# A tile scheduler that orders instructions by a finer simulator

## The chip, the core and the metric

The kernel runs on one core of one Trainium2 chip. A core has four compute engines that run side by side, each with its own list of instructions in a fixed order: TensorE (PE) multiplies matrices, with its loads of the fixed operand listed as PEld; VectorE (DVE) and ScalarE (ACT) work on elements; GpSimd (POOL) does some element work too. SyncE (SP) issues most transfers. An engine takes its instructions strictly as they are listed, and where one has to wait for another engine or for a transfer, all that stands behind it waits too. The time is that of one execution on the device in microseconds (us); of several runs the median is taken.

## The reference

The model has two layers, over 1024 tokens and 16 learned ones ahead of them (1040 in all), with 1024 features:

```python
merged = jnp.concatenate([rms_norm(o_sb, sb_norm_g), rms_norm(o_s5, s5_norm_g)], axis=-1)   # layer 0
return merged.astype(h.dtype) @ w_out
...
v_new = val_c - jnp.einsum('bhcd,bhde->bhce', kcd_c, state)                                 # layer 1
o_c = jnp.einsum('bhcd,bhde->bhce', qg_c, state) + jnp.einsum('bhcs,bhse->bhce', intra_c, v_new)
state = state * jnp.exp(gl_c)[..., None, None] + jnp.einsum('bhcd,bhce->bhde', kt_c, v_new)
...
return jnp.square(jax.nn.relu(h @ w1)) @ w2                                                 # after each mixer
```

Layer 0 mixes tokens by stick-breaking attention (8 heads of 64 features) and by an S5 state space model; layer 1 by a gated DeltaNet with 8 heads of 128 features: a causal convolution and a silu give queries, keys and values, a triangular system is solved within each chunk of tokens, and the state of a head goes from chunk to chunk. Behind each mixer stands an MLP of 4096 hidden features. All is in fp32.

## The kernel before

Features lie in the partitions, tokens along the rows. A large product (`unit`, L167) is cut into output tiles of 128 features by 336 to 352 tokens. Each operand is split into a high and a low part, and three matmuls (L174, L175, L176) for each of eight tiles of 128 input features add up in one of three PSUM banks named mm. Weights come by SP into wraw (two buffers), and DVE (L163) and POOL or DVE (L164) make whi and wlo of them.

The stages in the order of time, by the profile: projections and S5 of layer 0 and its attention (0 to 750 us), the MLP of layer 0 (to 1500), the DeltaNet mixer (1500 to 2250), and the MLP of layer 1. The mixer, `mixer1` (L1564), has two parts that matter here.

The preparation, about 1560 to 1850 us. For each head the products of `conv_in` (L1178) go from their PSUM bank to cx by DVE (L1189). `conv_silu` (L1195) makes cy of it: ACT scales (L1199), DVE adds three shifted copies (L1205), ACT applies the silu (L1206). `decays` (L1219) loads rows named grow, adds a mask (L1228 on POOL, L1229 on DVE) and takes exponentials (L1231 on ACT). `keys` (L1236) and `queries` (L1304) transpose cy on PE (L1251, L1266, L1315) and multiply it with itself (L1288, L1328). `solve` (L1340) inverts 128 triangular blocks of 32 x 32 on DVE, by 31 pairs of L1350 and L1351, once for heads 0 to 3 and once for heads 4 to 7; `combine` (L1384) makes inverses of 128 x 128 blocks of them.

The chain, about 1850 to 2175 us. `chain` (L1469) goes through the nine chunks of a head, one head after the other. A step takes the state S through PE (L1492), DVE (L1494, rho), PE (L1497), ACT (L1499, xc), PE (L1503) and DVE (L1508), which gives the next S; L1513 and L1514 on PE make the step's output. Each of these matmuls is of 128 x 128 fp32 values, which PE takes in two passes. Beside the chain stand the products for the gates and the values of later heads, `combine`, and `gated` (L1535, with transposes L1556).

The program writes its instructions out in Python: generators (strands) of one kind of work are stepped while another kind is emitted, with a clock of its own (`pause`, L111, and the constants C1, C2, C3 in the chain, J1 to J4 elsewhere). That gives a program order. The tile context at L1903 then decides the real order: it knows which instruction needs which, simulates the engines, and at each point lets an engine take, of the instructions that are ready in the simulated time, the one that comes first in program order. The buffers of the pools are given out as this goes. Which instruction counts as ready, and so what stands ahead of what on each engine, depends on the durations and delays that the simulator assumes. What one instruction waits for on the chip is set by the data and the buffers, not by the simulated times.

## Time and profile before

| | |
|---|---|
| runs, us | 3028.56, 3016.03, 3018.09 |
| median, us | 3018.09 |
| profiled execution, span from first to last instruction, us | 3011.3 |
| mean granted clock of PE in it | 0.948 |
| ACT busy, us (share) | 892.8 (30%) |
| POOL busy, us (share) | 864.6 (29%) |
| instructions of PE, DVE, ACT, POOL | 17628, 3158, 1934, 628 |

The span is the profiled execution's own time; the median of the runs is 6.8 us above it. Busy shares are means over the whole program, in which the stages differ, so a stage is read by a window of its own. A wait is listed with the engine and line that waited, and the last thing that it waited for. The granted clock is the share of PE's full clock that the chip let it have: at 0.50 a matmul takes twice its time.

### The profile page before, as it was taken

The page shows a single profiled execution, that of the slowest core. Times are in us where ns is not written, and L with a number is a line of the kernel's source. Part 1 is how long each engine was busy: PE and PEld are TensorE (multiplying, and loading weights), DVE is VectorE, ACT ScalarE, POOL GpSimd, SP SyncE. Part 2 cuts the span into 40 slices and gives each one's busy share as a digit, 9 for nine tenths or more (in the row PEclk, how much of TensorE's full clock was granted, in tenths as well). Part 3 has the DMA queues.
Part 4 walks back from the last instruction along what each step waited for, and adds up shares of the span by engine and source line. Part 5 has one row for each costly group of instructions (what it writes and reads, how often), then busy time and mean ns, then how long its engine had stood idle before and what let it go on. Part 6 is the DMA issues. An engine that isn't in the chain of part 4 may idle for free. (4 is left out here: it accounts for less than half of the span.)

```text
span 3011.3 us, 44561 instructions
## 1 busy us (share of the span) xinstructions
PE 2838.4 (94%) x17628; PEld 2685.8 (89%) x17628; DVE 1773.1 (59%) x3158; ACT 892.8 (30%) x1934; POOL 864.6 (29%) x628
## 2 busy tenths in 40 slices
PE   7899998999999999999896978999989999999998
PEld 7688667888999999999886978899988999999997
DVE  8633778667455555555646995545546455555555
ACT  4112566554311101111435423334434111111112
POOL 5551225225311221222522132211143222122123
PEclk9989567889999999999998999999999999999999
DMA  3435212134111111111426666453332111111113
GB/s 126 158 127 161 71 43 92 41 104 146 58 50 43 50 46 46 50 42 51 130 85 201 220 205 208 157 153 110 127 106 84 50 50 43 50 50 43 50 50 112
DMA packets 168289, 284.92 MB, mean 95 GB/s; under 512 B 40880, under 2 KB 108672, under 8 KB 168080
## 3 DMA queue, kind: packets, MB, share of 16 engines
q1 hardware_dynamic: 164192, 277.38, 28.8%
q10 hardware_dynamic: 3888, 4.69, 0.4%
q8 instruction: 139, 2.28, 0.3%
q14 instruction: 70, 0.57, 0.1%
HBM read 204.80 MB, written 77.21 MB: 94 GB/s over the span
## 5 line engine op out<-in xcount | busy, mean ns | idle before, releaser
L174 PE MATMUL mm<-ahi,whi 128*128 128x344 f32 (+2 forms) x2592 | 862.4, 333 | 33.5 <-DVE cx L1189 22.1
L164 POOL TENSOR_TENSOR wlo<-wraw,whi 128x1024 fp32r<-128x1024 f32 x181 | 439.5, 2430 | 1504.1 <-DVE whi L163 1138.1
L176 PE MATMUL mm<-ahi,wlo 128*128 128x344 f32 (+2 forms) x2592 | 844.9, 326 | 1.8 <-DVE wlo L164 1.8
L175 PE MATMUL mm<-hl,whi 128*128 128x344 f32 (+4 forms) x1920 | 619.1, 322 | 0.0
L174 PEld LDWEIGHTS mm<-ahi,whi 128*128 128x128 f32 x2592 | 497.2, 192 | 41.7 <-DVE cx L1189 23.3
L176 PEld LDWEIGHTS mm<-ahi,wlo 128*128 128x128 f32 x2592 | 497.0, 192 | 4.5 <-DVE wlo L164 2.9
L176 PE MATMUL mm<-hh,wlo 128*128 128x344 f32 (+4 forms) x1536 | 492.8, 321 | 2.9 <-POOL wlo L164 2.9
L408 DVE TENSOR_TENSOR acc<-mm,acc 128x344 f32<-128x344 f32 (+4 forms) x672 | 343.9, 515 | 253.4 <-PE mm L176 253.4
L174 PE MATMUL mm<-hh,whi 128*128 128x344 f32 (+4 forms) x1536 | 492.0, 320 | 0.1
L385 ACT ACTIVATE t<-t 128x344 f32<-128x344 f32 (+2 forms) x192 | 94.4, 492 | 1093.7 <-DVE t L384 1093.7
L175 PEld LDWEIGHTS mm<-hl,whi 128*128 128x128 f32 x1920 | 363.8, 189 | 1.3 <-issue 0.6
L175 PE MATMUL mm<-ml,whi 128*128 128x344 f32 (+2 forms) x1056 | 340.1, 322 | 0.7 <-DVE ml L227 0.7
L163 DVE CAST whi<-wraw 128x1024 fp32r<-128x1024 f32 x181 | 180.0, 997 | 196.7 <-PE mm L175 160.6
L176 PEld LDWEIGHTS mm<-hh,wlo 128*128 128x128 f32 x1536 | 289.2, 188 | 3.8 <-POOL wlo L164 3.5
L174 PEld LDWEIGHTS mm<-hh,whi 128*128 128x128 f32 x1536 | 289.5, 188 | 0.9 <-DVE acc L408 0.3
L227 DVE TENSOR_TENSOR hl<-t,hh 128x344 fp32r<-128x344 f32 (+2 forms) x192 | 162.2, 845 | 166.6 <-ACT hh L226 165.5
L175 PE MATMUL mm<-mh,whi 128*128 128x344 f32 (+2 forms) x768 | 246.8, 321 | 0.0
L175 PEld LDWEIGHTS mm<-ml,whi 128*128 128x128 f32 x1056 | 199.7, 189 | 1.1 <-DVE ml L227 1.0
L384 DVE SCALAR_TENSOR_TENSOR t<-mm,rb 128x344 f32<-128x344 f32 (+2 forms) x192 | 98.5, 513 | 121.0 <-PE mm L176 121.0
L175 PEld LDWEIGHTS mm<-mh,whi 128*128 128x128 f32 x768 | 144.6, 188 | 0.5 <-issue 0.2
L175 PE MATMUL mm<-hh,whi 128*128 128x344 f32 (+2 forms) x384 | 126.7, 330 | 0.0
L853 DVE TENSOR_TENSOR_SCAN keep<-keep,cst 128x400 f32<-128x400 f32 (+5 forms) x72 | 95.5, 1338 | 45.8 <-ACT keep L851 45.4
(425 smaller groups left out, 4530.0 us busy)
## 6 DMA issues: line engine op xcount, KB each, us to landing
wraw<-w SPq DMA_DIRECT2D x128, 512.0 KB, 3.5
wraw<-wino SPq DMA_DIRECT2D x32, 512.0 KB, 3.7
dm<-dmd SPq DMA_DIRECT2D x16, 520.0 KB, 4.8
hsd<-hs SPq DMA_DIRECT2D x48, 172.0 KB, 1.8
wraw<-wine SPq DMA_DIRECT2D x12, 512.0 KB, 3.7
wraw<-qkd SPq DMA_DIRECT2D x8, 520.0 KB, 3.6
acc<-acc SPq DMA_DIRECT2D x8, 520.0 KB, 4.6
dmd<-grow SPq DMA_DIRECT2D x8, 520.0 KB, 5.3
```

The lines of the kernel that those rows point to most:

```text
L163: nc.vector.tensor_copy(hi[:, :n], raw[:, :n])
L164: (nc.vector if fast else nc.gpsimd).tensor_sub(lo[:, :n], raw[:, :n], f(hi[:, :n]))
L174: nc.tensor.matmul(pt, wh, h[:, o:o + n], start=i == 0, stop=False)
L175: nc.tensor.matmul(pt, wh, l[:, o:o + n], start=False, stop=False)
L176: nc.tensor.matmul(pt, wl, h[:, o:o + n], start=False, stop=i == len(kts) - 1)
L227: (lo_eng or nc.vector).tensor_sub(lo, src, f(hi))
L384: nc.vector.scalar_tensor_tensor(t1[:, :n], pt, 0.0, st["rb"][:, o:o + n], op0=ALU.max, op1=ALU.mult)
L385: nc.scalar.activation(t2[:, :n], t1[:, :n], AF.Square)
L408: nc.vector.tensor_add(acc[m][:, o:o + n], pt, acc[m][:, o:o + n])
L853: v.tensor_tensor_scan(kp[:n, 0:L][:, ::-1], kp[:n, 0:L][:, ::-1], self.one_row[:n, :L], 1.0, op0=ALU.mult, op1=ALU.mult)
```

## The change

One argument of the tile context:

```diff
-    with _tile.TileContext(nc) as tc:
+    with _tile.TileContext(nc, schedule_with_timeline_sim=True) as tc:
```

(All other lines of the diff take out docstrings and comments; line numbers stay.) The scheduler uses its finer simulator, so the simulated times at which instructions become ready differ, and with them the order on each engine and the buffers given out. What is computed, and by which instructions, stays.

The order of PE's rows in the two MLPs (800 to 1400 and 2300 to 2900 us) is the same as before. Rows move in layer 0's mixer, and most in the DeltaNet mixer. ACT has 42 loads of a function table in place of 52. Three places are shown; in each row stand the line, the operation, output<-inputs by their names in the program with buffer numbers, the shape, and xN where rows of one kind follow each other.

The first is PE in the chain, one step and the start of the next. The names are those of `chain`: S is the state, ch a slot with a head's operands, rho and xc the values between the links. Before:

```order
L1492 MATMUL tr_18472<-S_18464,ch_18313 128x128
L174 MATMUL mm_18458<-ahi_13100,whi_18053 128x344
L175 MATMUL mm_18458<-hh_12777,whi_18053 128x344
L176 MATMUL mm_18458<-ahi_13100,wlo_18054 128x344
L174 MATMUL mm_18458<-ahi_13101,whi_18053 128x344
L175 MATMUL mm_18458<-hl_12778,whi_18053 128x344
L176 MATMUL mm_18458<-ahi_13101,wlo_18054 128x344
L1497 MATMUL tr_18496<-rho_18474,ch_18313 128x128
```

The same step in the changed order, on to the next products:

```order
L1492 MATMUL tr_18472<-S_18464,ch_18313 128x128
L1513 MATMUL ax_18510<-S_18464,ch_18319 128x128
L1497 MATMUL tr_18496<-rho_18474,ch_18313 128x128
L1503 MATMUL tr_18506<-xc_18498,ch_18316 128x128
L1514 MATMUL ax_18510<-xc_18498,ch_18316 128x128
L1492 MATMUL tr_18516<-S_18508,ch_18313 128x128
L1513 MATMUL ax_18510<-S_18508,ch_18319 128x128
L1497 MATMUL tr_18535<-rho_18518,ch_18313 128x128
L1503 MATMUL tr_18551<-xc_18537,ch_18316 128x128
L1514 MATMUL ax_18510<-xc_18537,ch_18316 128x128
L174 MATMUL mm_18759<-ahi_13098,whi_18526 128x352
L175 MATMUL mm_18759<-hh_12472,whi_18526 128x352
```

Product rows stood between the links of a step; now two whole steps follow each other with no product row, and the products stand behind them in a row.

The second is DVE near 1590 us, where the products of the convolution are evicted (L1189, cx from an mm bank) beside the convolution of other heads (L1205, cy) and the mask of the decays (L1229, grow). Before:

```order
L1229 TENSOR_TENSOR grow_14268<-grow_14268,cst_63 16x16
L163 CAST whi_14726<-wraw_14724 128x1024
L1189 TENSOR_TENSOR cx_14302<-mm_14304,rb_13107 128x352
L1189 TENSOR_TENSOR cx_14302<-mm_14351,rb_13107 128x344
L1205 SCALAR_TENSOR_TENSOR cy_14341<-cx_13696,gains_64,cy_14341 128x1040 x2
L1205 SCALAR_TENSOR_TENSOR cy_14363<-cx_13698,gains_64,cy_14363 128x1040
L1205 SCALAR_TENSOR_TENSOR cy_14341<-cx_13696,gains_64,cy_14341 128x1040
L1205 SCALAR_TENSOR_TENSOR cy_14363<-cx_13698,gains_64,cy_14363 128x1040
L1229 TENSOR_TENSOR grow_14381<-grow_14381,cst_63 16x16
L1189 TENSOR_TENSOR cx_14302<-mm_14388,rb_13107 128x344
```

And in the changed order:

```order
L1229 TENSOR_TENSOR grow_14268<-grow_14268,cst_63 16x16
L1189 TENSOR_TENSOR cx_14302<-mm_14304,rb_13107 128x352
L1189 TENSOR_TENSOR cx_14302<-mm_14351,rb_13107 128x344
L163 CAST whi_14932<-wraw_14930 128x1024
L1189 TENSOR_TENSOR cx_14302<-mm_14388,rb_13107 128x344
L1205 SCALAR_TENSOR_TENSOR cy_14341<-cx_13696,gains_64,cy_14341 128x1040 x3
L1205 SCALAR_TENSOR_TENSOR cy_14363<-cx_13698,gains_64,cy_14363 128x1040 x3
L1229 TENSOR_TENSOR grow_14381<-grow_14381,cst_63 16x16
```

The third eviction, of mm_14388, moved ahead of six rows L1205 and of the mask add of grow_14381; a weight's cast (whi_14932) moved ahead of it.

The third is DVE near 1760 us, in the second half's solve (sU_16026), where cx_16094 is evicted. Before:

```order
L1350 TENSOR_TENSOR sprod_16034<-sU_16026,sN_16025 128x192
L1351 TENSOR_TENSOR sU_16026<-sU_16026,sprod_16034 128x8x24
L1350 TENSOR_TENSOR sprod_16034<-sU_16026,sN_16025 128x207
L1351 TENSOR_TENSOR sU_16026<-sU_16026,sprod_16034 128x9x23
L1350 TENSOR_TENSOR sprod_16034<-sU_16026,sN_16025 128x220
L1351 TENSOR_TENSOR sU_16026<-sU_16026,sprod_16034 128x10x22
L1350 TENSOR_TENSOR sprod_16034<-sU_16026,sN_16025 128x231
L1189 TENSOR_TENSOR cx_16094<-mm_16096,rb_13107 128x352
L1189 TENSOR_TENSOR cx_16094<-mm_16126,rb_13107 128x344
```

And in the changed order:

```order
L1351 TENSOR_TENSOR sU_16026<-sU_16026,sprod_16034 128x4x28
L1205 SCALAR_TENSOR_TENSOR cy_16082<-cx_15477,gains_64,cy_16082 128x1040
L1320 TENSOR_SCALAR rq0_16039<-rq0_16039 128x8
L1189 TENSOR_TENSOR cx_16094<-mm_16096,rb_13107 128x352
L1351 TENSOR_TENSOR sU_15135<-sU_15135,sprod_15181 128x26x6
L1350 TENSOR_TENSOR sprod_15873<-U0_15835,N0_15834 8x55
L1350 TENSOR_TENSOR sprod_16034<-sU_16026,sN_16025 128x135
L1330 TENSOR_TENSOR dm2_15985<-tr_16059,dm2_15985 128x512
```

The first eviction of cx_16094 stood behind ten pairs of this solve and stands behind four now; rows of the first half's solve (sU_15135), which were done before this place, stand among them.

## The prediction

> **What bounds the kernel now.** The page comes first, its busy shares, to see which engine has no room.

> ```profile
> span 3011.3 us, 44561 instructions
> ## 1 busy us (share of the span) xinstructions
> PE 2838.4 (94%) x17628; PEld 2685.8 (89%) x17628; DVE 1773.1 (59%) x3158; ACT 892.8 (30%) x1934; POOL 864.6 (29%) x628
> ```

> PE is the bound: 2838.4 of 3011.3 us. The instructions stay the same, so the change can move the time in two ways only: by PE's idle time (173 us in all, the difference of these numbers) and by the clock that PE is granted. The next view, windows of PE, says in which stages either is to be had. Its columns are the window, its length, PE's busy time with its instructions, the granted clock, and the DMA share and rate.

> ```profile
> core 0: us, PE busy (x), PEclk, DMA share, GB/s
> 300.00:375.00 75.00, 69.00 (x263) 0.57 0.25 74
> 375.00:450.00 75.00, 69.22 (x325) 0.68 0.14 43
> 450.00:525.00 75.00, 67.02 (x334) 0.75 0.30 93
> 800.00:1400.00 600.00, 600.00 (x3785) 1.00 0.15 46
> 1560.00:1850.00 290.00, 235.16 (x1528) 0.93 0.67 210
> 1610.00:1615.00 5.00, 4.21 (x21) 0.66 1.07 310
> 1755.00:1760.00 5.00, 0.00 (x0) 0.50 0.51 170
> 1850.00:2175.00 325.00, 317.73 (x2332) 1.00 0.45 143
> 2300.00:2900.00 600.00, 600.00 (x3843) 1.00 0.16 49
> ```

> Four kinds of stage are seen. The MLPs (800 to 1400, 2300 to 2900) are full at full clock, and the order of PE's instructions in them is the same before and after: they give nothing and lose nothing. The preparation of the DeltaNet mixer (1560 to 1850: convolution, keys, decays, triangular solves) leaves PE idle for 290 - 235.16 = 54.8 us: here a better order can win. The chunk chain of that mixer (1850 to 2175) leaves 325 - 317.73 = 7.3 us at clock 1.00: here an order can only lose. Attention (300 to 525) is nearly full, but at 0.57 to 0.75 of the clock. The last view of this part, PE's waits (what waited, for what; us in total, times, longest), names the waits in the two stages of the mixer.

> ```profile
> PE mm L174 <- DVE cx L1189: 22.1, 4, 12.0
> ...
> PE tr L1315 <- ACT cy L1206: 12.6, 4, 5.7
> ...
> PE tr L1251 <- ACT cy L1206: 9.3, 3, 7.8
> ...
> PE tr L1497 <- DVE rho L1494: 3.0, 5, 0.9
> ...
> PE tr L1492 <- DVE S L1508: 2.4, 3, 1.1
> ```

> The first three lie in the preparation, the last two in the chain, where they come to 5.4 us in all.

> **The chain: the term that decides.** One step of the chain goes L1492 on PE, L1494 on DVE, L1497 on PE, L1499 on ACT, L1503 on PE, L1508 on DVE, and on to the next L1492. L1513 and L1514 hang on it without being on it. The trace shows one step in which PE came close to waiting (start, length, engine and line):

> ```profile
> 1858.61 0.39 PE L1492 MATMUL tr<-S,ch 128*128 128x128 f32 x2
> ...
> 1858.83 0.39 PE L1513 MATMUL ax<-S,ch 128*128 128x128 f32 x2
> ...
> 1859.04 0.35 DVE L1494 SCALAR_TENSOR_TENSOR rho<-tr,dge,vn 128x128 f32<-128x128 f32 x1 [1.48 <-PE tr L1492]
> ...
> 1859.44 0.49 PE L1497 MATMUL tr<-rho,ch 128*128 128x128 f32 x2
> ...
> 1860.03 0.37 ACT L1499 ACTIVATE xc<-tr,b 128x128 f32<-128x128 f32 x1 [1.75 <-PE tr L1497]
> ...
> 1860.45 0.49 PE L1503 MATMUL tr<-xc,ch 128*128 128x128 f32 x2
> ...
> 1860.98 0.35 DVE L1508 SCALAR_TENSOR_TENSOR S<-S,dgegl,tr 128x128 f32<-128x128 f32 x1 [1.59 <-PE tr L1503]
> ```

> From the start of one link on PE to the earliest start of the next it takes 1859.44 - 1858.61 = 0.83 us for L1492 to L1497, 1860.45 - 1859.44 = 1.01 for L1497 to L1503, and for L1503 to the next L1492 up to the end of L1508 (1861.33) and the same 0.05 that lies between L1494's end and L1497: 0.93. A link that starts on an idle PE lasts 0.49 and not 0.39, so the first becomes 0.93 there. On a full PE one such matmul takes 1858.83 - 1858.61 = 0.22.

> Whether PE waits is a matter of what stands between two links in its order. Before, product matmuls (L174 to L176) stand between nearly all of them: none of the 64 steps has L1492 and L1497 with fewer than three rows between, none L1497 and L1503. In the changed order the products stand in bursts of some 24, and between the bursts the chain stands bare: 36 times of 64 L1492 is followed by L1513 alone and then L1497; 38 times of 64 L1497 by L1503 with nothing between; 34 times of 56 L1503 by L1514 alone and then the next L1492. Such a link leaves PE idle for its delay less what PE issues in it:
> - L1492 to L1497: 0.93 - 0.44 = 0.49, 36 times, 17.6 us
> - L1497 to L1503: 1.01 - 0.22 = 0.79, 38 times, 30.0 us
> - L1503 to L1492: 0.93 - 0.44 = 0.49, 34 times, 16.7 us

> That is 64.3 us, and with links 0.10 shorter, as on a full PE, 53.5. Off it go the 5.4 us that PE waits there now: 48 to 59 us, of which 54 is taken, between the two, as some bare links start at the end of a burst. DVE and ACT may add to it where another row stands ahead of L1494 or L1499; the bounds stay.

> The clock is a second cost there. The bare stretches keep PE about half busy, as no stretch of the chain does before. The nearest row, 1610 to 1615, is of matmuls of the same size with short waits: 4.21 of 5 us busy at 0.66. At that clock three links of 0.39 become 0.59, 0.2 x 3 x 36 = 22 us; at full clock nothing. 5 is taken, nearer the chain's own 1.00, with 0 and 22 as ends. [...]

> **The preparation: what is won.** The four longest waits of PE that the order touches, and two rows of DVE ahead of the first:

> ```profile
> 1591.41 2.14 DVE L1229 TENSOR_TENSOR grow<-grow,cst 16x16 f32<-16x16 f32 x1 [5.73 <-DMA grow<-grow]
> ...
> 1593.48 0.50 DVE L1189 TENSOR_TENSOR cx<-mm,rb 128x344 f32<-128x344 f32 x1
> ...
> 1594.03 0.65 PE L174 MATMUL mm<-ahi,whi 128*128 128x344 f32 x1 [5.31 <-DVE cx L1189]
> ...
> 1627.52 1.12 PE L1251 MATMUL tr<-cst,cy 128*128 128x128 f32 x4 [7.77 <-ACT cy L1206]
> ...
> 1737.01 1.02 PE L1315 MATMUL tr<-cst,cy 128*128 128x128 f32 x4 [4.39 <-ACT cy L1206]
> ...
> 1758.65 0.37 DVE L1350 TENSOR_TENSOR sprod<-sU,sN 128x207 f32<-128x207 f32 x1
> ...
> 1761.20 0.66 PE L174 MATMUL mm<-ahi,whi 128*128 128x352 f32 x1 [11.99 <-DVE cx L1189]
> ```

> At 1594 PE waits for a PSUM bank whose eviction (L1189) stands on DVE behind the mask add L1229, which waits 5.73 us for a DMA. In the changed order that eviction stands ahead of the add: 5.3 us go. At 1761 the evictions of cx_16094 stand behind ten pairs of the second solve (L1350, L1351); in the changed order they stand among its first pairs, each behind the one before by ten rows or so. About 3 us are left of the 12.0: 9.0 go. The waits for ACT's silu (L1251, L1315; 12.6 + 9.3 = 21.9 us) are covered by more products here and by fewer there; a third, 7.3, is taken. Against it stands the first half's solve, whose last rows now stand behind some 20 rows of the second half's, about 0.37 us each, 7 us, and the chain of the first head needs it; a product burst covers most, 2 is taken. Together -5.3 - 9.0 - 7.3 + 2 = -20 us. The ends are -55 (all the idle time) and +7 (nothing won, the solve late).

> **Attention and the rest.** In attention the same rows are grouped otherwise; the share of rows by which the clock seems to go (scores of 64 rows against products of 128) is spread more evenly, but not larger or smaller. 0 is taken, with the bounds from the windows above: at 0.9 throughout, the three windows would shrink by 75 x (1 - 0.57/0.9) + 75 x (1 - 0.68/0.9) + 75 x (1 - 0.75/0.9) = 58 us; at 0.57 throughout, they would grow by 14 + 24 = 38. ACT's table loads fall from 52 to 42; ACT does not bound anything but the silu waits counted above.

> The sum: +54 + 5 - 20 + 0 = +39 on the profiled 3011.3, 3050 us. The median of the runs shown is 3018.1, 6.8 above the span, so the median after is 3057.

> **The rivals.**
> - *The preparation gives all of its idle time back.* PE's order there is no longer held by DVE's evictions, and the 54.8 us go whole: +54 + 5 - 55 = +4, 3022 us. For it: DVE's order changes most there. Against: a stage with PE at 81% also waits for DMA round trips (5.73 us above), which no order shortens. It decides (not slower by 0.5%, 15 us) once over 44 of the 55 go.
> - *Attention keeps a higher clock*, the rival on the other side. Spread scores keep the windows of 300 to 525 at 0.9: 58 us less, +39 - 58 = -19, 2999 us. For it: the clock there does change with the mix (0.57, 0.68, 0.75). Against: the mix is as large as before. From 24 us on (a clock of some 0.75 on average) the kernel is not slower by 0.5%, from 54 on it is faster.
> - *The clock falls in the bare chain*: 22 for 5, and half-clock starts of the bursts, about 1.5 us for some 8 of them: +39 + 17 + 12 = +68, 3086 us.
> - *The chain's links are covered after all*, because the bare stretches overlap waits that PE would have had for weights: 0 for 54, -15, 3003 us. The window of the chain at 317.73 of 325 speaks against it.

> **How the numbers follow.** About 0.5%, 15 us, is what a measurement of this kernel can tell from no change: below 3003 is faster, above 3033 slower. The forecast has 0.50, slower. The full gain in the preparation 0.19 and part of the covered chain 0.03, the same. Attention's clock 0.12 and the other part of the covered chain 0.02, faster. The clock in the chain 0.14, slower. So faster 0.14, same 0.22, slower 0.64. Three fourths of the faster cases are left out below, and few above: 3005 to 3095.

> **What would show it.** In the changed profile PE's waits for L1494, L1499 and L1508 together should rise from 5.4 to between 45 and 65 us, and PE's busy share in the chain should fall from 98% to about 85%. If they stay under 20, the chain term is wrong. PE's wait for cx L1189 should fall from 22.1 to about 8 us; if it stays, the gain is wrong. The granted clock between two bursts of the chain tells the third rival, that of 300 to 525 the second. The MLPs should show 600 of 600 us again. Two things would make the prediction wrong that no row bounds: a new wait for a weight's cast, as whi (L163) moves against the evictions on DVE, and a DMA that is issued later on its queue.

## The result and the profile after

| | before | after |
|---|---|---|
| median, us | 3017.06 (4 runs, 3013.88 to 3028.56) | 3151.7 (4 runs, 3135.15 to 3157.88) |
| profiled execution, span, us | 3011.3 | 3146.2 |
| mean granted clock of PE in it | 0.948 | 0.928 |

The changed kernel is slower: the ratio is 1.0442, with a 95% interval of 1.0413 to 1.047. The forecast, 3057, had the side right and less than a third of the size; the time is outside its range (3005 to 3095).

The busy shares of the page after, for comparison with those of before:

```profile
span 3146.2 us, 44540 instructions
...
PE 2882.4 (92%) x17628; PEld 2723.0 (87%) x17628; DVE 1720.6 (55%) x3158; ACT 873.4 (28%) x1924; POOL 902.4 (29%) x628
```

PE's instructions are as many as before, but they took 44 us longer in all (2882.4 for 2838.4), and PE idles 263.8 us instead of 173. So the loss of 134.9 us is of two kinds: some 91 us of idle time and some 44 us of matmuls that lasted longer.

To see where, both executions were divided at the PE instructions that begin or end a stage (the length of each stage, us):

| stage | before | after | difference |
|---|---|---|---|
| opening | 327.5 | 316.5 | -11.0 |
| attention and the rest of mixer 0 | 383.8 | 391.6 | +7.8 |
| residual and norm behind mixer 0 | 54.4 | 71.0 | +16.6 |
| MLP 0 | 701.6 | 696.6 | -5.1 |
| residual and norm behind MLP 0 | 74.1 | 85.5 | +11.5 |
| preparation of mixer 1 | 278.0 | 261.8 | -16.2 |
| start of the chain | 32.6 | 46.4 | +13.7 |
| chain | 348.3 | 447.0 | **+98.7** |
| residual and norm behind mixer 1 | 92.5 | 107.5 | +15.0 |
| MLP 1 | 674.8 | 671.2 | -3.7 |
| last norm | 34.8 | 41.6 | +6.8 |

They come to +134. The chain is three quarters of it. The four residual stages cost 49.9 us, less the 8.8 that the MLPs behind them give back: 41. The other stages together give back 6. Where the preparation ends and the start of the chain begins is a choice, since their rows are interleaved: divided behind the same number of PE instructions, these two rows read -11.1 and +8.5. Their sum, about -2.5, doesn't depend on it.

The windows of PE after, over the stages of the prediction and then in pieces of 10 us in the chain (window, its length, PE's busy time with its instructions, granted clock, DMA share and rate):

```profile
825.00:1425.00 600.00, 600.00 (x3785) 1.00 0.15 48
300.00:375.00 75.00, 70.04 (x297) 0.64 0.28 78
375.00:450.00 75.00, 63.30 (x315) 0.75 0.21 72
450.00:525.00 75.00, 71.31 (x321) 0.68 0.19 57
1869.40:2316.40 447.00, 392.13 (x2480) 0.90 0.31 99
1960.00:1970.00 10.00, 9.98 (x75) 1.00 0.80 220
1970.00:1980.00 10.00, 7.53 (x46) 0.97 0.31 97
1980.00:1990.00 10.00, 8.10 (x35) 0.50 0.25 95
1990.00:2000.00 10.00, 8.95 (x48) 0.50 0.60 194
2000.00:2010.00 10.00, 9.46 (x53) 0.66 0.16 25
2010.00:2020.00 10.00, 9.83 (x71) 1.00 0.13 52
```

The same window of before, between the same two instructions with the same 2480 matmuls, reads:

```profile
1852.10:2200.40 348.30, 341.03 (x2480) 1.00 0.41 133
```

So in the chain PE idles 54.9 us instead of 7.3, +47.6, and is busy 392.13 us instead of 341.03, +51.1. The clock is 0.50 in ten stretches of this window, 92.2 us together, and 1.00 in the rest. The sum over the ten:

```profile
sum 92.18, PE 76.76; mean PE 7.68
```

At 0.50 a product of 352 columns starts every 0.29 us where it starts every 0.16 us at 1.00 (1.8 times, not twice), and one of the small 128 x 128 matmuls, of two passes, every 0.43 us (L1513 to L1514 in the kernel with four bare steps in a row) where it starts every 0.22; so close to half of the 76.76, some 38 us by estimate from these times, is what the clock cost in busy time. The other 13 of the 51.1 us are, by estimate, links that start on an idle PE: such a link takes 0.49 us by itself, where a full PE spends 0.22 on it (both numbers are in the prediction). The longest of the ten stretches:

```profile
1979.46:2006.77 27.31, 23.28 (x105) 0.50 0.39 116
```

PE is busy for 85% of it and yet has half its clock. Product rows stand only in its last 2.6 us (from 2004.14); what runs ahead of them are four steps of the chain, bare of products, with transposes (L1556) and rows of `combine` (L1408, L1415, L1424). Over all ten stretches, each row counted until the next one starts, the steps' own rows (L1492, L1497, L1503, L1513, L1514) have 40 of the 77 us, the small matmuls of `combine` and `gated` 16, and the products 21. (The clock falls within PE's longest wait for L1508, 3.0 us; whether such a wait is needed for it is a question for the experiments.)

PE's waits over the whole run after (what waited, for what; us in total, times, longest):

```profile
PE mm L174 <- DVE cx L1189: 30.7, 5, 9.7
PE ax L219 <- DVE diag L212: 28.4, 6, 7.5
PE tr L1503 <- ACT xc L1499: 21.2, 39, 1.5
...
PE tr L1492 <- DVE S L1508: 11.9, 27, 3.0
PE mm L174 <- DVE t L384: 11.3, 2, 5.7
...
PE tr L1497 <- DVE rho L1494: 9.1, 29, 0.8
PE mm L174 <- ACT acc L1060: 8.7, 1, 8.7
```

The three links of the chain come to 42.2 us (5.4 before), a little under the 45 to 65 that the prediction named. The chain's idle time holds one more long wait that is no link: the last row, 8.7 us once, at 2286, near the chain's end. The wait for cx L1189, which was to fall from 22.1 to 8, rose to 30.7. And a wait that the prediction doesn't name stands second: L219 for diag (L212), 28.4 us. It belongs to the residual stages, where a norm's scale goes from DVE's reciprocal (L204) through diag to a small matmul (L219) that spreads it over the partitions. The timeline of the one behind mixer 0, after, shows what it waits behind (start, length, engine, line, tiles, count):

```profile
731.76 3.96 DVE L317 SCALAR_TENSOR_TENSOR acc<-acc,gains,ax 128x344 f32<-128x344 f32 x8 [3.73 <-PE ax L219]
...
736.06 0.17 DVE L204 RECIPROCAL rs_r<-rs_r 88x4 f32<-88x4 f32 x1
736.14 3.04 DVE L318 TENSOR_TENSOR hs<-acc,hs 128x344 f32<-128x344 f32 x7
...
741.40 1.23 DVE L212 TENSOR_TENSOR diag<-cst,rs_r 88x352 f32<-88x352 f32 x1
...
742.77 1.51 PE L219 MATMUL ax<-diag,cst 88*128 88x352 f32 x2 [5.74 <-DVE diag L212]
```

The reciprocal is done at 736.23 and diag starts at 741.40, behind seven rows of L318 and two of L230: 5.2 us for a tile that PE waits for. In the order of before the same place reads:

```profile
737.76 0.16 DVE L204 RECIPROCAL rs_r<-rs_r 88x4 f32<-88x4 f32 x1
...
738.25 0.74 DVE L212 TENSOR_TENSOR diag<-cst,rs_r 88x352 f32<-88x352 f32 x1
```

There diag follows behind one eviction (L1078, 0.48 us), and L317, L318 and L230 go on piece by piece for one feature tile after the other; in the changed order all eight L317 come first, then all L318.

### The profile page after: what moved, and what is told of

Same layout as the page of the kernel before. It is cut to its first block, busy times and chain, and to the rows that moved or that the text cites. A ratio compares the mean times of both kernels' runs of the same rounds, so it can differ in the third digit from the quotient of the medians.

```text
span 3146.2 us, 44540 instructions
## 1 busy us (share of the span) xinstructions
PE 2882.4 (92%) x17628; PEld 2723.0 (87%) x17628; DVE 1720.6 (55%) x3158; ACT 873.4 (28%) x1924; POOL 902.4 (29%) x628
## 5 line engine op out<-in xcount | busy, mean ns | idle before, releaser
L174 PE MATMUL mm<-ahi,whi 128*128 128x344 f32 (+2 forms) x2592 | 856.5, 330 | 72.8 <-DVE cx L1189 30.7
L164 POOL TENSOR_TENSOR wlo<-wraw,whi 128x1024 fp32r<-128x1024 f32 x181 | 452.3, 2506 | 1581.3 <-DVE whi L163 1199.8
L176 PE MATMUL mm<-ahi,wlo 128*128 128x344 f32 (+2 forms) x2592 | 847.0, 327 | 0.6 <-DVE wlo L164 0.6
L174 PEld LDWEIGHTS mm<-ahi,whi 128*128 128x128 f32 x2592 | 501.6, 194 | 82.0 <-DVE cx L1189 33.0
L176 PEld LDWEIGHTS mm<-ahi,wlo 128*128 128x128 f32 x2592 | 500.5, 193 | 2.5 <-DVE wlo L164 1.0
L174 PE MATMUL mm<-hh,whi 128*128 128x344 f32 (+4 forms) x1536 | 492.9, 321 | 2.8 <-DVE acc L408 2.8
L176 PE MATMUL mm<-hh,wlo 128*128 128x344 f32 (+4 forms) x1536 | 491.1, 320 | 0.0
L174 PEld LDWEIGHTS mm<-hh,whi 128*128 128x128 f32 x1536 | 288.5, 188 | 5.7 <-DVE acc L408 5.3
L176 PEld LDWEIGHTS mm<-hh,wlo 128*128 128x128 f32 x1536 | 288.6, 188 | 0.3
L227 DVE TENSOR_TENSOR hl<-t,hh 128x344 fp32r<-128x344 f32 (+2 forms) x192 | 154.9, 807 | 175.9 <-ACT hh L226 165.6
L163 DVE CAST whi<-wraw 128x1024 fp32r<-128x1024 f32 x181 | 130.1, 732 | 208.3 <-PE mm L175 200.8
L242 POOL TENSOR_TENSOR ssq<-ssq,sq 128x344 f32<-128x344 f32 (+2 forms) x84 | 99.7, 1187 | 100.6 <-ACT sq L241 94.3
```

Of the source, the lines that this page charges most:

```text
L163: nc.vector.tensor_copy(hi[:, :n], raw[:, :n])
L164: (nc.vector if fast else nc.gpsimd).tensor_sub(lo[:, :n], raw[:, :n], f(hi[:, :n]))
L174: nc.tensor.matmul(pt, wh, h[:, o:o + n], start=i == 0, stop=False)
L176: nc.tensor.matmul(pt, wl, h[:, o:o + n], start=False, stop=i == len(kts) - 1)
L227: (lo_eng or nc.vector).tensor_sub(lo, src, f(hi))
L242: nc.gpsimd.tensor_add(st["ssq"][:, o:o + n], st["ssq"][:, o:o + n], sq[:, :n])
```

## The experiments

All eleven kernels compute the whole reference. They hold instructions of one or more engines, each engine for itself, in a given order, taken from the other kernel or written for the question, by edges between instructions that follow each other on the same engine. Such an edge sets the order of issue and adds no wait. The scheduler places everything else as it likes, so other stages move by a few us in each of these kernels; the readings below go by stage, divided as in the table above. The edit that is common to all:

```diff
+def pin(nc, tc, order):
+    by = {i.name: i for i in nc.cur_bb.bb.instructions}
+    free = mybir.DependencyInfo(mybir.DependencyClass.NoSync, mybir.DependencyReason.DATA)
+    for text in order:
...
+        for a, b in zip(names, names[1:]):
+            tc.add_manual_dep(by[b], a, free, reason="pin")
...
+            pin(nc, tc, ORDER)
```

What differs is ORDER, the lists of instructions, and the flag in the tile context. Where a list holds whole stages, the diff gives it in words. The letters of the theories are those of the expectations, which were written before each run.

**Is it the chain's order on PE?** First the changed kernel with PE's rows of the chain as before; then the kernel before with PE's rows of the chain as in the change. The diff at one step of the first, on PE:

```diff
 L1503 MATMUL tr<-xc,kt_16923 128x128
 L1415 MATMUL tr<-U,X 64x64 x8
-L175 MATMUL mm<-hl,whi 128x344
-L176 MATMUL mm<-ahi,wlo 128x344
...
 L1492 MATMUL tr<-S,ch 128x128
+L174 MATMUL mm<-ahi,whi 128x344
+L175 MATMUL mm<-hl,whi 128x344
+L176 MATMUL mm<-ahi,wlo 128x344
+L174 MATMUL mm<-ahi,whi 128x344
+L1497 MATMUL tr<-rho,ch 128x128
```

> The changed kernel, with TensorE's instructions from the last products of the preparation to the first of the output product held in the order that they had before; every other order is the scheduler's. Theory A (the bare links on TensorE are the cause of what the chain lost, 99 us between the same two instructions): the stretch from L174-176 at 1869 us on takes 348 us again and not 447, TensorE's waits for L1494, L1499 and L1508 fall from 42 to under 10 us, the granted clock there goes back to 1.00, and the whole is 80 to 105 us shorter than the changed kernel, some 3055 us. Rival B (the orders of VectorE, ScalarE and the transfers make the chain late, and TensorE's order only follows them): under 30 us shorter, with TensorE idle elsewhere in the stretch.

Measured: 3062.25 us, ratio to before 1.0118 (1.0045 to 1.019). The chain's window:

```profile
1874.00:2236.00 362.00, 346.21 (x2480) 0.99 0.39 124
```

The chain falls from 447.0 to 362.0 us, and the time by 89 us with PE's order in one stage alone. That is 85 of the 98.7 us.

The second has the same lists the other way round (`-` and `+` of the diff above change places, in the kernel before).

> The kernel before, with TensorE's instructions of the chain alone held in the changed order (the others keep their order but for what follows from it). Theory A: 90 to 105 us longer than before, of which 45 to 55 are idle time of TensorE and about as much a granted clock that falls from 1.00 to about 0.90 in the chain. Theory A with the clock's loss coming from elsewhere (the late start of the chain, other rows): 45 to 60 longer at a clock of 1.00. Rival B: under 30 longer.

Measured: 3135.44 us, ratio 1.0359 (1.0281 to 1.0438).

```profile
1856.70:2319.10 462.40, 395.97 (x2480) 0.89 0.31 100
```

The chain alone takes 114 us more than before, by an idle time of 66.4 us and a clock of 0.89. That is more than in the change, as products wait 12.7 us here for an eviction of z (L1530), against 1.1 there. So PE's order in the chain is enough for the loss, and 85 of the 98.7 us need it; where the other 13.7 come from was not tried.

**The residual stages.** The changed kernel with DVE's rows of the four residual stages as before, then with PE's rows of them as well. The diff on DVE at the first norm:

```diff
+L204 RECIPROCAL rs_r<-rs_r 86x4
+L212 TENSOR_TENSOR diag<-cst,rs_r 86x344
+L317 SCALAR_TENSOR_TENSOR acc<-acc,gains,ax 128x344 x2
+L318 TENSOR_TENSOR hs<-acc,hs 128x344
...
-L317 SCALAR_TENSOR_TENSOR acc<-acc,gains,ax 128x352 x8
-L318 TENSOR_TENSOR hs<-acc,hs 128x352 x2
```

> The changed kernel, with VectorE's instructions in the four residual stages (output products and norms behind each mixer and MLP) held in the order that they had before. Theory C (in the changed order VectorE takes up all eight tiles of a chunk line by line, L317 eight times, L318 eight times, then L230, so that the diagonal L212 and the first pieces of the next product come late): the four stages, which lost 17, 12, 13 and 6 us, win back 35 to 48 us together; TensorE's waits for diag L212 fall from 28 to about 10 us. Rival D (TensorE's own order there, or the transfers, are the cause): under 15 us.

Measured: 3137.71 us, ratio 1.0367 (1.028 to 1.0454), so 14 us less than the change; the two intervals overlap, so the reading rests on the stages. Against before, the stage behind mixer 0 is at +1.1 with +5.9 in the MLP behind it, that behind MLP 0 at -2.9, that behind mixer 1 at +1.5, the last norm at +6.7. That is 12 of the 41 us: 29 came back with DVE's order. Not all of it is seen in the time, since the chain's start became 6 us longer and mixer 0 about 10 us longer than in the changed kernel. PE's wait for diag, in its list of waits, is half of what it was:

```profile
PE ax L219 <- DVE diag L212: 14.3, 7, 4.3
```

The next kernel adds PE's rows of the same stages:

```diff
-    ORDER = DVE of four stages
+    ORDER = DVE of four stages, PE of four stages
```

> The changed kernel, with the instructions of VectorE and of TensorE in the four residual stages held in the order that they had before. With VectorE alone held, 30 of the 39 us that these stages lost came back; the last stage kept its 6.8 us and the first 7 of 11.5. Theory C (the orders of the two engines together are the whole cause): the four stages come within 5 us of before, the kernel is about 35 to 45 us shorter than the changed one, some 3110 us. Rival D (ScalarE's, GpSimd's order or the transfers cause the rest): no more than the 30 us.

Measured: 3125.55 us, ratio 1.0344 (1.0311 to 1.0377). The MLP's +5.9 became +1.1 and the last norm's +6.7 became +0.1; behind mixer 1 +7.2 is left. DVE's order was the larger cause in these stages, PE's the smaller.

**Both causes together.** The changed kernel with PE's rows from the start of the chain on, and PE's and DVE's of the residual stages, as before:

```diff
-    ORDER = DVE of four stages, PE of four stages
+    ORDER = DVE of four stages, PE of four stages, PE of the chain and its start
```

> The changed kernel, with TensorE held in the order of before from the start of the chain to its end and both TensorE and VectorE in the residual stages. If the causes named so far add up (chain 85 of 99 us, residual stages 39, start of the chain up to 14), it takes 3010 to 3030 us, no more than 0.4% from before, and what is left of the changed order (the opening, attention, the preparation) neither wins nor loses. If something else costs too, it stays above 3045.

Measured: 3032.69 us (10 runs), ratio 1.004 (1.0022 to 1.0059), just above what was expected. The two causes add up to nearly the whole loss. The chain is 13.5 us longer than before, the preparation 20.7 shorter, and the start of the chain 16.6 longer. So of the preparation's gain, the one term of the forecast that was for the change, 4 us are left at the point where the chain begins.

**Is that gain worth anything alone?** The kernel before with the rows of PE, DVE and ACT in the preparation (1541 to 1800 us) as in the change, the solve's rows left free. On PE, for instance:

```diff
-L1115 MATMUL tr<-fold,abrow 128x16 x5
+L1115 MATMUL tr<-fold,abrow 128x16 x2
 L174 MATMUL mm<-ahi,whi 128x344
-L175 MATMUL mm<-hh,whi 128x344
 L1115 MATMUL tr<-fold,abrow 128x16 x3
```

> The kernel before, with the instructions of TensorE, VectorE and ScalarE in the preparation (what ran from 1541 to 1800 us) held in the changed order, but for the rows of the triangular solve on VectorE, which stay free. The changed kernel won 16 us up to there and lost 14 in the start of the chain that follows. If the gain is the order of evictions and convolution, and the loss that of the solve, 8 to 18 us shorter than before (0.3 to 0.6%). If gain and loss are one thing (what is done earlier is done at the cost of what the start of the chain needs), within 5 us of before.

Measured: 3037.99 us (8 runs), ratio 1.006 (1.0042 to 1.0078). Both expectations missed: it is 16 us slower than the runs of before beside it. The three parts of the preparation are at +9.7, +9.9 and -5.9, the start of the chain at +13.5 and the chain at -3.6. With the solve's order left free, the preparation doesn't gain 16 us but loses 14, so this kernel doesn't repeat what the change did there, and it can't tell where the late start comes from. That cause stays open; the next kernel excludes one candidate, DVE's order in that place. It is the changed kernel with DVE's rows from 1795 to 1900 us as before:

```diff
-L1189 TENSOR_TENSOR cx<-mm,rb 128x344
...
+L1350 TENSOR_TENSOR sprod<-sU,sN 128x192
+L1351 TENSOR_TENSOR sU<-sU,sprod 128x24x8
...
+L1189 TENSOR_TENSOR cx<-mm,rb 128x344
```

> The changed kernel, with VectorE's instructions around the end of the preparation and the start of the chain (what ran from 1795 to 1900 us before) held in the order that they had before. The changed kernel lost 24 us there, in 1812 to 1869 us. Theory E (VectorE's rows of the late solve, of L1330 and of the convolution are in the wrong order for TensorE): 15 to 25 us shorter. Rival F (the data come late, as the solve of the first half is interleaved with the second's already from 1720 us on): under 8 us.

Measured: 3155.7 us, ratio 1.0426 (1.0325 to 1.0527): no different from the change, as the rival F had it. The start of the chain stays late, +18.6. In the kernel with both causes undone, PE waits there for the queries' silu, in its list of waits:

```profile
PE tr L1315 <- ACT cy L1206: 14.5, 3, 9.4
```

One of the three, 9.4 us, is at the start of the chain: a convolution that is issued later on ACT and DVE is the nearest cause, but that was not tried by itself.

**What does a bare link cost, and what takes the clock down?** Three kernels of before, with the products between links moved and nothing else. In the first, the products between L1497 and L1503 stand behind L1503, so that one link of a step is bare, 46 times:

```diff
 L1497 MATMUL tr<-rho,ch 128x128
-L174 MATMUL mm<-ahi,whi 128x344
-L175 MATMUL mm<-hl,whi 128x344
-L176 MATMUL mm<-ahi,wlo 128x344
 L1503 MATMUL tr<-xc,ch 128x128
+L174 MATMUL mm<-ahi,whi 128x344
+L175 MATMUL mm<-hl,whi 128x344
+L176 MATMUL mm<-ahi,wlo 128x344
```

> The kernel before, with the product matmuls that stood between L1497 and L1503 moved behind L1503, in all steps of the chain where nothing else is moved: 46 links of this one kind stand bare, and the products of a step stay dense. At 0.69 to 0.79 us a link, 32 to 36 us of idle time. If the clock follows what TensorE does over a few microseconds, it stays at 1.00 in the chain, and the kernel is 30 to 40 us longer than before. If each wait of this kind takes the clock down, it is 0.95 or less there and the kernel 50 to 65 us longer.

Measured: 3065.05 us, ratio 1.0144 (1.0112 to 1.0176); the link in its list of waits, then the chain's window:

```profile
PE tr L1503 <- ACT xc L1499: 24.2, 46, 1.1
```

```profile
1863.90:2246.50 382.60, 351.89 (x2480) 0.99 0.38 121
```

24.2 / 46 = 0.53 us of waiting a link, where the prediction had 0.79. But the whole chain is 34.3 us longer, 0.75 a link, since a link on an idle PE also lasts longer (0.49 us for 0.39, as in the prediction's step): the price was about right, only a part of it shows as busy time. The clock stays at 0.99, though PE waits 46 times.

In the second, 32 of the 64 steps are bare, one at a time, with products ahead of each and behind it:

```diff
+L174 MATMUL mm<-ahi,whi 128x336
+L175 MATMUL mm<-hh,whi 128x336
 L1492 MATMUL tr<-S,ch 128x128
 L1513 MATMUL ax<-S,ch 128x128
-L174 MATMUL mm<-ahi,whi 128x336
-L175 MATMUL mm<-hh,whi 128x336
 L1497 MATMUL tr<-rho,ch 128x128
-L176 MATMUL mm<-ahi,wlo 128x336
-L174 MATMUL mm<-ahi,whi 128x336
-L175 MATMUL mm<-hl,whi 128x336
 L1503 MATMUL tr<-xc,ch 128x128
```

> The kernel before, with every second step of the chain (32 of 64) bare: its product matmuls are moved ahead of its L1492 or behind its L1514, so that each bare step stands alone between some 3 us of dense products, where the changed order has runs of up to six bare steps and bursts of 24 rows and more. About 29 links L1492 to L1497 at 0.49 us and 26 links L1497 to L1503 at 0.79, less what other rows cover, some 25 to 35 us of idle time. If the length of the bare run takes the clock down, it stays at 0.98 or more in the chain and the kernel is 25 to 40 us longer than before. If the number of bare links does, the clock is about 0.94 and the kernel 45 to 60 us longer.

Measured: 3065.07 us, ratio 1.0144 (1.0112 to 1.0176).

```profile
PE tr L1497 <- DVE rho L1494: 20.3, 29, 2.0
...
PE tr L1503 <- ACT xc L1499: 15.0, 27, 1.6
```

```profile
1856.80:2251.30 394.50, 356.60 (x2480) 0.98 0.37 117
```

The clock is as the theory of the run's length had it; the chain's loss, 46.2 us, is above the 25 to 40 that went with it.

In the third as many steps are bare, but four in a row, with their products half ahead of the first and half behind the last:

```diff
+L174 MATMUL mm<-ahi,whi 128x336
...
 L1492 MATMUL tr<-S,ch 128x128
 L1513 MATMUL ax<-S,ch 128x128
 L1497 MATMUL tr<-rho,ch 128x128
 L1503 MATMUL tr<-xc,ch 128x128
 L1514 MATMUL ax<-xc,ch 128x128
 L1492 MATMUL tr<-S,ch 128x128
```

> The kernel before, with 32 of the 64 steps of the chain bare as in the run with single bare steps, but four in a row in each head: the product matmuls of the four steps stand half ahead of the first and half behind the last. 57 bare links against 52 there, which had 35 us of waits for the links, a clock of 0.98 in the chain and 46 us lost in it. If the length of a bare run takes the clock down, the clock in the chain is 0.90 to 0.95 here and the chain loses 60 to 80 us, with waits of 30 to 42 us. If the number of bare links or their idle time does, the clock stays at 0.97 or more and the loss at 40 to 52 us.

Measured: 3078.58 us, ratio 1.0191 (1.0152 to 1.023).

```profile
PE tr L1497 <- DVE rho L1494: 14.6, 25, 3.2
PE tr L1503 <- ACT xc L1499: 13.2, 26, 0.7
...
PE tr L1492 <- DVE S L1508: 2.1, 8, 0.7
```

```profile
1851.80:2263.00 411.20, 378.50 (x2480) 0.93 0.34 112
```

This pair shows that the grouping matters. PE waits less for the links in the third kernel (29.9 us in 59 waits) than in the second (35.3 in 56), and yet the chain is 16.7 us longer, for its busy time is 378.50 and not 356.60. So it isn't the sum of the waits or their number, but how the bare steps stand. The clock is at 0.50 for 58 us of this chain, for 17 in the second kernel and, by its mean of 0.99, for some 7 in the first. One run of four, in the third kernel, on PE:

```profile
2056.20 0.49 PE L1497 MATMUL tr<-rho,ch 128*128 128x128 f32 x2 [0.44 <-DVE rho L1494]
2057.20 0.49 PE L1503 MATMUL tr<-xc,ch 128*128 128x128 f32 x2 [0.52 <-ACT xc L1499]
...
2058.13 0.49 PE L1492 MATMUL tr<-S,ch 128*128 128x128 f32 x2
2059.06 0.49 PE L1497 MATMUL tr<-rho,ch 128*128 128x128 f32 x2 [0.44 <-DVE rho L1494]
2060.07 0.55 PE L1503 MATMUL tr<-xc,ch 128*128 128x128 f32 x2 [0.52 <-ACT xc L1499]
2060.41 0.64 PE L1513 MATMUL ax<-S,ch 128*128 128x128 f32 x2
```

The run began with an L1492 at 2051.89. No gap in it is over 0.52 us, and L1513, 0.39 us at full clock, takes 0.64 at its end: the clock falls at 2060.37, after some 8 us without a product. So here it fell without a long wait. In the second kernel two single gaps of nearly four times that length stand among products, and the clock falls behind one of them only:

```profile
2018.73 0.49 PE L1497 MATMUL tr<-rho,ch 128*128 128x128 f32 x2 [1.93 <-DVE rho L1494]
...
2020.74 0.49 PE L175 MATMUL mm<-hh,whi 128*128 128x344 f32 x1
```

```profile
2164.03 0.49 PE L1497 MATMUL tr<-rho,ch 128*128 128x128 f32 x2 [2.00 <-DVE rho L1494]
...
2165.36 0.39 PE L1513 MATMUL ax<-S,ch 128*128 128x128 f32 x2
```

```profile
2056.96:2060.37 3.41, 2.20 (x12) 1.00 0.81 259
2060.37:2063.78 3.41, 3.41 (x19) 0.50 0.86 284
```

```profile
2017.15:2020.56 3.41, 1.31 (x9) 1.00 0.39 144
2020.56:2023.97 3.41, 3.41 (x14) 0.50 0.46 154
2160.51:2163.92 3.41, 1.53 (x11) 1.00 0.46 119
```

In the changed kernel's chain 103 such windows are at full clock. In ten of them PE is busy for 24 to 64% of the time (0.84 to 2.18 us), and behind each of the ten the clock is 0.50; in the other 93 it is busy for 65% or more, and behind none. In the chain of before PE is busy for 65% or more in all 101, and the clock never falls. Of the changed chain's windows without any product row, 9 are among the ten and 16 among the 93, so the kind of rows doesn't decide there: what goes with the fall is how much of such a window PE idles. In the second kernel the window at 2160.51 is against it: PE is busy for 45% of it and keeps its clock. The run of four above, 15.7 us from its first L1492 to the next product (at 2067.57), spans more than four such lengths; a single bare step takes less than one, some 2.4 us by an estimate from the prediction's link times (0.93 + 1.01 + 0.49). The way back is another matter: of the changed chain's 27 windows at half clock, six have product rows for 77% of the time or more, and behind each of them the clock is 1.00; of the other 21, with product rows for a quarter of the time at most, four have 1.00 behind them. So bare steps, once the clock was down, mostly kept it down here.

**The opening.** Its 11 us were the largest gain of the change behind the preparation's. The kernel before with the first 300 us of all engines in the changed order:

```diff
-    ORDER = none
+    ORDER = PE, DVE, ACT, POOL and SP of 0 to 300 us, as in the change
```

> The kernel before, with all engines' instructions of the first 300 us held in the changed order. The changed kernel was 11 us ahead at 327 us and lost 8 of them in attention. If these are two things, 5 to 11 us shorter than before (0.2 to 0.4%); if attention gives back what the opening wins, within 4 us of before.

Measured: 3017.76 us (10 runs), ratio 0.9984 (0.9963 to 1.0004). No gain that can be told from none: the opening is some 3.5 us shorter than before, not 11, and the rest of mixer 0 some 6 longer. Why the 11 us didn't come back is open. No version that was run beats the kernel before.

## Why the prediction was right or wrong

- **The chain as the term that decides: right.** Its place, its mechanism and the sign were as the prediction put them, and the pair of kernels with the chain's order exchanged shows it. The links were taken as 54 us. They waited 36.8 us more than before (42.2 less 5.4), and by estimate 13 us more went into links that last longer on an idle PE: 50. The nearness of the idle time, +47.6, to 54 is in part luck, as it holds the wait of 8.7 us for acc (L1060), which no term names. PE's busy share in the chain was to be about 85%; it is 392.13 / 447 = 88%.
- **The clock in the chain: here the sum failed first.** The prediction took 5, "nearer the chain's own 1.00, with 0 and 22 as ends", without a row for the choice of 5; the clock cost 38 us of busy time. Its row, 0.66 at 1610 to 1615, is a mean over 5 us. In the chain the clock was 0.50 for 92 us, and what ran at it was more than the three links of a bare step (0.2 x 3 x 36): L1513 and L1514, the small matmuls beside the steps, and 21 us of products. So the end of 22 was no bound. The third rival saw this mechanism, with a chance of 0.14. Its 12 us for "half-clock starts of the bursts" were near what the products lost (half of 21), though the 1.5 us that it took for each start came from no row, and no run shows that time by itself; its 22 for the steps were too few (half of 40 + 16).
- **"Attention and the rest: 0". Right for attention, wrong for the rest: here it failed a second time.** Mixer 0 in all is at -3.2 us, and the mean clock of its three windows is 0.69 for 0.67, where the second rival needed 0.9, so that rival fell. That the clock there goes by the share of the scores was the author's estimate: before, 95, 84 and 70 of the instructions in the three windows are scores (L845 to L847), at a clock of 0.57, 0.68 and 0.75; after, 78, 90 and 63, at 0.64, 0.75 and 0.68, so it isn't shown. But the residual stages, which no sentence of the prediction prices, lost 41. Their order on DVE had changed as much as the chain's on PE, from tile by tile to line by line, and the comparison of orders would have shown it.
- **The preparation, -20: worth almost nothing.** With the start of the chain it comes to -2.5 us. The prediction allowed 2 us for a late first head; the late start took most of the gain, and its cause is open. The wait for cx L1189 was to fall to 8 and rose to 30.7, but not all of it lies here: in the preparation it fell from 22.1 to 12.8, of which 9.7 are one eviction that still stands behind a mask add that waits for its DMA, and 12.9 came in the residual stage behind MLP 0.
- **The MLPs, 600 of 600: right.**

Term by term, measured for forecast: links 50 for 54, clock 38 for 5, other waits in the chain 11 for 0, preparation with the start of the chain -2.5 for -20, residual stages 41 for 0, mixer 0 -3 for 0. That is +134 for +39.

## What to carry to other kernels

When a scheduler or a reordering bunches the links of a dependent chain, count a bare run twice: once for the latency of its links, and once for the clock, which in the run here was at 0.50 for 92.2 of the chain's 447 us and mostly stayed there until products came again. Bare links apart from each other cost about what their latency promised: 0.75 us each in the kernel with one bare link a step, for 0.79. And compare the orders of all stages, the short ones between two large ones as well: a row that one engine needs next (here a norm's scale) may have moved behind a whole row of others that nobody waits for.
